# First layer's MoE routing and row transposes: VectorE in place of ScalarE and GpSimd, and another order

## The chip, the cores and the metric

The kernel runs on one core of a Trainium2 chip. Its engines work side by side, each through its own list of instructions: TensorE (PE; its weight loads are shown as PEld), VectorE (DVE), ScalarE (ACT), GpSimd (POOL) and SyncE (SP), which only starts transfers. The metric is the device time of one execution in microseconds. The kernel before took 1183.16 us, the median of three runs (1179.98, 1183.16 and 1186.79).

## The reference

A two-layer backbone over 256 latent and 256 context tokens, 512 rows of 1024 numbers in all. The first layer mixes with attention, the second with a state-space model (SSM); each is followed by a mixture of experts (MoE), in which every row goes to the best group of four and the best two of its eight experts:

```python
def moe_tokens(xt, gw, gb, rw, rb, w_gate, w_up, w_down):
    g_logits = xf @ gw + gb
    _, g_idx = lax.top_k(g_logits, 1)
    p_group = jnp.sum(softmax(g_logits) * g_onehot, axis=-1, keepdims=True)
    e_sel = jnp.einsum('sge,sg->se', e_logits, g_onehot)
    e_val, e_idx = lax.top_k(e_sel, MOE_TOP_K)
    w_top = jax.nn.softmax(e_val, axis=-1) * p_group
    ...
    hid = jax.nn.silu(xt @ w_gate) * (xt @ w_up) * combine
    return hid @ w_down
...
    h = h + m[2] * y                        # mixer's output
    h = h + m[5] * hier_moe(modulate(rms_norm(h, norm2_g[layer]), m[3], m[4]), *moe_p)
```

The rows xt that enter the experts are the normed and modulated rows: h times 1/rms, times a row a2, plus a row b2.

## The kernel before

The rows are held as four tiles of 128, t = 0 to 3. The attention's output projection makes one tile of H after another (L742 and L743), and the steps of the first layer's routing are woven in behind each tile (list at L747 to L751, pairs of step and tile). The steps are: 0 and 1 (`half`, `prep`, L834 to L853: sums of squares, 1/rms, the modulated rows xn and their transfer to `xd` in device memory), 2 (`logits` and `choose`, L858 to L906, the group and the two experts of every row), 3 (`places`, L909, each row's slot in its expert and in the last tile the index list `gidx`, L954), 4 (`worth`) and 5 (`weights`, L973 to L996, the gate weights put into a table by TensorE). For t = 0 to 2 the rows are made by VectorE (L849, L851), for the last tile by two ScalarE copies (L845), and a product and a sum of GpSimd for each half of 512 columns (L846, L847).

`gidx` lets GpSimd gather rows from `xd`: `gather(j)` (L1180) fetches the 128 slots of expert pair j, 512 KB, into one of two buffers xg0 and xg1. Between the gathers of pairs 0 and 1 stands `overflow` (L1018 to L1030), nine VectorE instructions and a memset that count the blocks of rows beyond the experts' capacity; all engines read the count (L1046) and branch on it (L1047). The branch isn't taken with these inputs.

Then 16 pairs are worked on. Of pair j, `rows` turns the gathered rows (8 transposes, L329, and two copies L1232), `up(0)` and `up(1)` are the two halves of the first product (ph, L1251), ScalarE and VectorE make the hidden values `hd` (L1259, L1260), `hidT` turns them (L1237, copy hT L1239), `down` is the second product (py, L1277) and a scatter of the result (L1280). `pipeline` (L189) runs these steps with a lag in rounds for each. In a round stand: rows of a pair, hidT and the aside work of the pair two before, up of the pair one before, down of the pair two before. The aside work is the making of the next layer's SSM matrices: VectorE products (L1610, L1611, W by a helper, L149) that wait for transfers `Rd` of GpSimd's queue, and small matmuls on TensorE (vt, kp, pk: L1624 to L1638).

Weights come as 1 MB transfers through a ring of buffers (L1334 to L1369), started by SyncE in the order of use: 13 are in flight before the branch or just behind it, the next ones wait until TensorE has finished with a buffer. Within a block a scheduler sets the order of each engine's instructions; steps written through `TE_`, `VP_`, `P_` and `A_` keep the order in which they are written.

The second layer's MoE (from about 948 us) has another scheme without gathers; its pairs keep their order.

Of the kernel before, what the change touches and what calls it, by code (L numbers as in the profile page):

```python
# [130 lines left out]
def bc(ap, shape):  # L131
    return ap.to_broadcast(shape)
# [3 lines left out]
def hybrid(ctx: ExitStack, tc: tile.TileContext, A, out, taps=None, stop=None):  # L136
    nc = tc.nc
    taps = taps or {}
    V_ = nc.vector
# [232 lines left out]
    def attention(moe_mods, disp_open):  # L372
# [350 lines left out]
        with ExitStack() as wctx:  # L723
            wq = wctx.enter_context(tc.tile_pool(name="wq", bufs=1))
            wo = Splitter(wq, [A["wout"][i] for i in range(2)], "wo", 4, (V_, nc.gpsimd))
            wo.half(0, 0)
            wo.half(0, 1)
            for hf in range(2):
                for j in range(4):
                    s = slice(j * 128, (j + 1) * 128)  # L730
                    if (hf, j) == (0, 2):
                        setup()
                    if (hf, j) == (0, 3):
                        wo.half(1, 0)
# [12 lines left out]
                    for i, t in (((0, 0),), ((1, 0), (0, 1)), ((2, 0), (1, 1), (0, 2)),  # L747
                                 ((0, 3), (1, 2), (3, 0), (4, 0), (5, 0), (2, 1)))[j]:
                        steps[i](t)
            for i, t in ((1, 3), (3, 1), (4, 1), (5, 1), (2, 2), (3, 2), (4, 2), (5, 2), (2, 3), (3, 3), (4, 3), (5, 3)):  # L750
                steps[i](t)  # L751
        octx.close()

# [50 lines left out]
    def dispatch_open(layer, Ht, M, VB, tag, xn2=None):  # L804
# [4 lines left out]
        T = M.T  # L809
# [6 lines left out]
        V_.tensor_copy(on, oneb)  # L816
        ohs = dp.tile([128, T, 32], BF, name="ohs")
        M.tabs = [bank(tag, name="ptab") for _ in range(2)]
        xns = {}

        halves = [slice(512 * i, 512 * i + 512) for i in range(2)]
        sums = dp.tile([128, T, 2], F32, name="sums")

        nt = 2 if layer == 0 else 1
        rws, C = M.scores if layer else (dp.tile([128, 8, nt, 36], F32, name="rws"), dp.tile([128, 36], F32, name="rc"))
# [7 lines left out]

        def half(t, hf):  # L834
            row_ss(sums[:, t], hf, Ht[t][:, halves[hf]])

        def prep(t):
            half(t, 1)
            turn(HT[t % 2], Ht[t], 0)
            rstd = rms(sums[:, t, 0:1], 1, D, "rstd", sums[:, t, 1:2])  # L840
            xn = dp.tile([128, D], F32, tag="xn2", bufs=2, name="xn2") if xn2 is None else xn2[:, t]
            xns[t] = rstd
            for s in halves:
                if t == T - 1:
# [64 lines left out]
        def places(t):  # L909
# [5 lines left out]
            V_.tensor_scalar(e64, m, -float(CAP), float(32 * CAP), op0=OP.mult, op1=OP.add)  # L915
            RV = M.RV[:, t]
            tm, p, ov = st("tm", [2, 32]), st("p", [2]), st("ov", [2])
            par, oj = st("par", [2]), st("oj", [2, NJ])
            ov2 = oh.rearrange("p k (a b) -> p k a b", b=per)
            if M.dma:  # L920
                V_.tensor_reduce(par, ov2[:, :, :, 1], axis=AX.X, op=OP.add)
# [10 lines left out]

            pe = st("pe", [2])
            V_.scalar_tensor_tensor(pe, in0=par, scalar=64.0 if M.dma else 1.0, in1=p, op0=OP.mult, op1=OP.add)
            eqm = st("eqm", [2, 128], FR)
            for k in range(2):
                V_.tensor_scalar(eqm[:, k], iota, pe[:, k:k + 1], None, op0=OP.is_equal)
            R = st("R", [2, 3 * NJ], FR)
            if M.dma:
                nc.gpsimd.tensor_mul(R[:, :, 0:16], oj, bc(cst[:, C_IDK + 2 * t:C_IDK + 2 * t + 2, None], [128, 2, 16]))  # L940
                for k in range(2):
# [31 lines left out]
        def weights(t):  # L973
# [19 lines left out]
            if t == T - 1:  # L993
                wt = st("wt", [N])
                nc.scalar.copy(wt, M.tabs[1][:, 0:N])
                V_.tensor_add(M.WS, wt, M.tabs[1][:, N:2 * N])  # L996
        return setup, lambda t: half(t, 0), prep, logits, choose, places, worth, weights

    def evac(mp, M, py, ws, Yh, Yl, hf):

# [16 lines left out]

    def overflow(M, e, pool):  # L1018

        nb, x, inc, one = (pool.tile([128, 32], F32, name=n) for n in ("nb", "nbx", "nbi", "nb1"))  # L1020
        CAP = M.CAP
        e.tensor_scalar(nb, M.cnt, float(CAP), None, op0=OP.is_gt)
        for i in range(1, 4):
            e.tensor_scalar(x, M.cnt, float(CAP + 128 * i), None, op0=OP.is_gt)
            e.tensor_add(nb, nb, x)
        nc.gpsimd.memset(one, 1.0)
        e.tensor_tensor_scan(inc, one, nb, 0.0, op0=OP.mult, op1=OP.add)
        tot = pool.tile([1, 1], I32, name="nbt")
        e.tensor_copy(tot, inc[0:1, 31:32])
        M.over = nb, inc, tot  # L1030

    def spill(layer, T, M, Ht, ring):

        NB, CAP = 16, M.CAP
        with ExitStack() as fctx:
# [9 lines left out]
            nb, inc, tot = M.over  # L1045
            nblk = nc.values_load(tot[0:1, 0:1], min_val=0, max_val=NB)  # L1046
            with tc.If(nblk > 0):  # L1047
                lo = st([128, 32]) if M.dma else M.a2[:, 128:160]
                V_.tensor_sub(lo, inc, nb)
                ge = fp.tile([128, NB, 32], F32, tag="ow", bufs=2, name="ge")  # L1050
                V_.tensor_tensor(ge, bc(iotb[:, 0:NB][:, :, None], [128, NB, 32]),
# [111 lines left out]
    def experts(Ht, M, VB, load, aside):  # L1163
# [3 lines left out]
        with ExitStack() as ectx:  # L1167
# [43 lines left out]
            def pair(j):  # L1211
                st = {}
# [892 lines left out]
```

## Time and profile before

| | before |
|---|---|
| median of three runs | 1183.16 us |
| the profiled execution's own time | 1182.01 us |
| its span in the trace | 1180.2 us |
| busy: PE / DVE / ACT / POOL | 77% / 53% / 30% / 23% |
| moved by DMA | 317.14 MB, 269 GB/s on the mean |

The span is the stretch from the first to the last instruction in the trace; the time of the execution is 1.8 us longer. Busy shares are means over stages with different limits. In the page, PE is busy in most slices, and the DMA engines are near full in two stretches: the first layer's MoE (about 400 to 665 us) and the second layer's (from about 948 us to the end). Between the last row of H (375.70 us) and the first gather, TensorE and the DMA engines have little to do for some 20 us, but for transfers of weights that run until about 389 us.

### The profile page before, as it was taken

Reading aid. Unit: us, or ns where it says so; the run is one execution under the profiler, and the core shown is the slowest. Engines: PE = TensorE matmul, PEld = TensorE weight load, DVE = VectorE, ACT = ScalarE, POOL = GpSimd, SP = SyncE. Lnnn points to the kernel's source line nnn. Section 1 sums busy time; section 2 is a strip of 40 time slices with the busy share of each in tenths; the row PEclk is TensorE's granted clock in tenths of the full one; section 3 lists DMA queues with packets and bytes.
Section 4 is the critical chain, followed back from the end, with each engine's and each line's share of the span. In section 5 each row is a group of like instructions: output and inputs, shape, how many; then the busy total and the mean of one; then the engine's idle time right before and its main releaser. Section 6 shows DMA issues by size and latency. Waiting matters only on the chain. (4 is left out here: it accounts for less than half of the span.)

```text
span 1180.2 us, 15033 instructions
## 1 busy us (share of the span) xinstructions
PE 913.9 (77%) x5398; PEld 477.3 (40%) x5398; DVE 625.1 (53%) x1649; ACT 350.4 (30%) x705; POOL 270.7 (23%) x347
## 2 busy tenths in 40 slices
PE   3577989999898599787897896965289597776663
PEld 0365866434487333232332245712078441121110
DVE  1778794677549516553530038988847841111113
ACT  2332224756533212111120113713754320000001
POOL 0533321322422423132126305000045300000001
PEclk9798999999999599898898997986589797788797
DMA  9782222665653699998899974382356689999994
GB/s 289 269 217 71 72 72 72 215 230 201 233 224 137 226 377 408 415 372 332 345 415 344 406 268 122 144 335 107 141 175 257 249 324 420 420 420 420 420 420 166
DMA packets 54814, 317.14 MB, mean 269 GB/s; under 512 B 8587, under 2 KB 9627, under 8 KB 21712
## 3 DMA queue, kind: packets, MB, share of 16 engines
q1 hardware_dynamic: 42910, 285.49, 63.6%
q0 software_dynamic: 10080, 26.92, 6.2%
q10 hardware_dynamic: 1746, 3.73, 0.9%
q8 instruction: 44, 0.72, 0.2%
q14 instruction: 34, 0.28, 0.1%
HBM read 305.80 MB, written 19.94 MB: 276 GB/s over the span
## 5 line engine op out<-in xcount | busy, mean ns | idle before, releaser
L1251 PE MATMUL ph<-w,xgT 128*64 128x512 f32 x512 | 140.9, 629 | 10.0 <-DMA w<-in_gu 10.0
L248 PE MATMUL pm<-wmod,cs 128*32 128x512 f32 x352 | 52.0, 683 | 60.0 <-DMA wmod<-in_modw 51.8
L339 PE MATMUL pp<-wlo,xo 128*128 128x512 f32 (+1 forms) x224 | 88.5, 395 | 5.2 <-POOL wlo L360 5.0
L338 PE MATMUL pp<-whi,xo 128*128 128x512 f32 (+1 forms) x224 | 90.0, 402 | 1.3 <-ACT whi L358 1.3
L340 PE MATMUL pp<-whi,xo 128*128 128x512 f32 (+1 forms) x224 | 87.7, 392 | 0.0
L1277 PE MATMUL py<-w,hT 128*64 128x512 f32 x224 | 76.7, 646 | 0.9 <-DMA w<-in_dn 0.8
L1251 PEld LDWEIGHTS ph<-w,xgT 128*64 128x64 f32 x512 | 38.8, 141 | 78.2 <-issue 57.8
L360 POOL TENSOR_TENSOR wlo<-win,whi 128x1024 fp32r<-128x1024 f32 (+1 forms) x20 | 44.9, 2272 | 79.5 <-ACT whi L358 79.5
L1251 PE MATMUL ph<-w,xn 128*32 128x512 f32 x256 | 43.7, 771 | 23.7 <-DMA w<-in_gu 23.6
L1260 DVE TENSOR_TENSOR a<-a,ph 128x256 f32<-128x256 f32 x8 | 3.4, 422 | 101.1 <-ACT a L1259 101.1
L339 PEld LDWEIGHTS pp<-wlo,xo 128*128 128x128 f32 x224 | 44.6, 199 | 15.6 <-POOL wlo L360 7.8
L1260 DVE TENSOR_TENSOR hd<-sg,ph 128x256 f32<-128x256 f32 x16 | 6.7, 418 | 81.4 <-ACT sg L1259 81.4
L1303 PE MATMUL py<-w,m 128*32 128x512 f32 x256 | 42.5, 747 | 9.3 <-DMA w<-in_dn 8.7
L582 DVE TENSOR_REDUCE nm<-sc 128x1 f32<-128x512 f32 (+1 forms) x64 | 35.1, 551 | 26.2 <-PE sc L615 15.7
L338 PEld LDWEIGHTS pp<-whi,xo 128*128 128x128 f32 x224 | 44.8, 200 | 10.2 <-ACT whi L358 2.2
L340 PEld LDWEIGHTS pp<-whi,xo 128*128 128x128 f32 x224 | 44.4, 198 | 8.6
L248 PEld LDWEIGHTS pm<-wmod,cs 128*32 128x32 f32 x352 | 9.4, 115 | 88.6 <-issue 48.0
L1251 PE MATMUL ph<-w,xg 128*32 128x512 f32 x256 | 32.9, 640 | 14.4 <-DMA w<-in_gu 13.1
L363 POOL TENSOR_TENSOR wlo<-glu,whi 128x512 fp32r<-128x512 f32 x16 | 26.7, 1698 | 69.4 <-ACT whi L358 67.1
L1003 DVE SCALAR_TENSOR_TENSOR Yl<-py,WS,Yh 128x512 fp32r<-128x512 f32 x18 | 13.4, 750 | 54.5 <-ACT Yh L1002 41.9
L585 ACT ACTIVATE e<-sc,nm 128x512 f32<-128x512 f32 (+1 forms) x64 | 37.4, 586 | 12.7 <-DVE nm L582 8.4
L1277 PEld LDWEIGHTS py<-w,hT 128*64 128x64 f32 x224 | 22.1, 146 | 43.5 <-issue 40.4
(492 smaller groups left out, 1953.7 us busy)
## 6 DMA issues: line engine op xcount, KB each, us to landing
w<-in_gu SPq DMA_DIRECT2D x127, 1024.0 KB
w<-in_dn SPq DMA_DIRECT2D x62, 1024.0 KB
wmod<-in_modw SPq DMA_DIRECT2D x42, 1024.0 KB
win<-in_win SPq DMA_DIRECT2D x8, 1024.0 KB
glu<-in_glu SPq DMA_DIRECT2D x8, 1024.0 KB
yd<-in_zero SPq DMA_DIRECT2D x1, 4096.0 KB
wo<-in_wout SPq DMA_DIRECT2D x4, 1024.0 KB
w<-yd SPq DMA_DIRECT2D x4, 1024.0 KB
```

The source lines that it names most:

```text
L248: nc.tensor.matmul(pm[32 * i:32 * i + 32, :], lhsT=cs[:, kk, :], rhs=w(kk), start=kk < 4, stop=kk >= 4)
L338: nc.tensor.matmul(o, lhsT=lh, rhs=rh, start=start, stop=False)
L339: nc.tensor.matmul(o, lhsT=lh, rhs=rl, start=False, stop=False)
L340: nc.tensor.matmul(o, lhsT=ll, rhs=rh, start=False, stop=stop)
L360: self.engines[i].tensor_tensor(lw, w[:, 2 * i:2 * i + 2, :], hi.bitcast(F32), op=OP.subtract)
L363: e.tensor_tensor(lw[:, k], w[:, 2 * i + k, :], hi.bitcast(F32)[:, k], op=OP.subtract)
L582: V_.tensor_reduce(nm, sp_[:, :n], axis=AX.X, op=OP.max, negate=True)
L585: nc.scalar.activation(e[:, :n], sp_[:, :n], AF.Exp, bias=nm, scale=1.0, accum_out=z)
L1003: V_.scalar_tensor_tensor(Yl[:, s], in0=py, scalar=ws, in1=Yh[:, s].bitcast(F32), op0=OP.mult, op1=OP.subtract)
L1251: nc.tensor.matmul(ph[s, :], lhsT=st["x"][:, 4 * q + kk, s], rhs=g[:, i, kk % 2] if M.dma else g[:, i], start=(q, kk) == (0, 0), stop=(q, ...
L1277: nc.tensor.matmul(py[s, :], lhsT=st["hT"][:, fk, s], rhs=d[i][:, fk, hf * 512:hf * 512 + 512], start=fk == 0, stop=fk == 1)
L1303: nc.tensor.matmul(py[s, :], lhsT=st["hT"][:, fk, s], rhs=r, start=fk == 0, stop=fk == 1)
```

## The change

1. The last tile's rows. `half` of tile 3 now also makes the product of H and a2 (VectorE, into two new tiles `xlast`), and a new step 6, `lastrows`, multiplies by 1/rms and adds b2, one VectorE instruction for each half, each half with its own transfer of 256 KB to `xd`. The copies of ScalarE and the four instructions of GpSimd are gone.
2. The order of the steps. `weights` of tiles 1 and 2 stand behind the choices of tile 3; the small tiles that they read (oj, eqm, R) have two buffers.
3. `overflow` is three VectorE instructions; the rest of the counting is inside the branch.
4. In the first MoE the `rows` of a pair stand between the two halves of `up` of the pair before, and not at the head of the round.

```diff
-            for i, t in ((1, 3), (3, 1), (4, 1), (5, 1), (2, 2), (3, 2), (4, 2), (5, 2), (2, 3), (3, 3), (4, 3), (5, 3)):
+            for i, t in ((1, 3), (3, 1), (4, 1), (2, 2), (3, 2), (4, 2), (2, 3), (6, 3), (5, 1), (3, 3), (4, 3), (5, 2), (5, 3)):
                 steps[i](t)
...
+        xlast = [sm.tile([128, 512], F32, tag=n, bufs=1, name="xlast") for n in ("mrow", "gb")] if layer == 0 else None
...
         def half(t, hf):
             row_ss(sums[:, t], hf, Ht[t][:, halves[hf]])
+            if layer == 0 and t == T - 1:
+                V_.tensor_mul(xlast[hf], Ht[t][:, halves[hf]], M.a2[:, halves[hf]])
...
             rstd = rms(sums[:, t, 0:1], 1, D, "rstd", sums[:, t, 1:2])
+            xns[t] = rstd
+            if layer == 0 and t == T - 1:
+                rstds.append(rstd)
+                return
...
+        def lastrows(t):
+            for x, s in zip(xlast, halves):
+                V_.scalar_tensor_tensor(x, in0=x, scalar=rstds[0], in1=M.b2[:, s], op0=OP.mult, op1=OP.add)
+                nc.gpsimd.dma_start(M.xd[t * 128:(t + 1) * 128, s], x)
...
-            par, oj = st("par", [2]), st("oj", [2, NJ])
+            par, oj = st("par", [2]), st("oj", [2, NJ], bufs=2 if M.dma else 1)
...
-        nb, x, inc, one = (pool.tile([128, 32], F32, name=n) for n in ("nb", "nbx", "nbi", "nb1"))
-        CAP = M.CAP
-        e.tensor_scalar(nb, M.cnt, float(CAP), None, op0=OP.is_gt)
-        for i in range(1, 4):
-            e.tensor_scalar(x, M.cnt, float(CAP + 128 * i), None, op0=OP.is_gt)
-            e.tensor_add(nb, nb, x)
-        nc.gpsimd.memset(one, 1.0)
-        e.tensor_tensor_scan(inc, one, nb, 0.0, op0=OP.mult, op1=OP.add)
-        tot = pool.tile([1, 1], I32, name="nbt")
-        e.tensor_copy(tot, inc[0:1, 31:32])
+        x, sm_, tot = pool.tile([128, 4, 32], F32, name="nbx"), pool.tile([128, 1], F32, name="nbs"), pool.tile([1, 1], I32, name="nbt")
+        e.scalar_tensor_tensor(x, in0=bc(M.cnt[:, None, :], [128, 4, 32]), scalar=float(M.CAP),
+                               in1=bc(cst[:, C_J:C_J + 4, None], [128, 4, 32]), op0=OP.subtract, op1=OP.is_gt)
+        e.tensor_reduce(sm_, x.rearrange("p a b -> p (a b)"), axis=AX.X, op=OP.add)
+        e.tensor_copy(tot, sm_[0:1])
...
-                return (rows, hidT, lambda: aside(j), lambda: up(0), lambda: back(0), lambda: up(1), lambda: back(1), down)
+                s = (rows, hidT, lambda: aside(j), lambda: up(0), lambda: back(0), lambda: up(1), lambda: back(1), down)
+                return s[1:4] + s[:1] + s[4:] if M.dma else s
...
-            pipeline([pair(j) for j in range(NJ)], (0, 2, 2, 1, 3, 1, 3, 2))
+            pipeline([pair(j) for j in range(NJ)], (2, 2, 1, 0, 3, 1, 3, 2) if M.dma else (0, 2, 2, 1, 3, 1, 3, 2))
```


The lines R and eqm have the same edit as oj; the counting that moved into the branch is not shown.

The list of GpSimd behind the last memset of a gather buffer, first before, then after. xn2 is the tile of the last rows, b2 of L1580 and L1591 a tile of SSM constants, R the gate weights' right-hand sides:

```order
L869 MEMSET xg1_3053 128x1024
L846 TENSOR_TENSOR xn2_3601<-xn2_3601,H1_95 128x512
L847 TENSOR_TENSOR xn2_3601<-xn2_3601,b2_96 128x512
L846 TENSOR_TENSOR xn2_3601<-xn2_3601,H1_95 128x512
L981 TENSOR_TENSOR R_3758<-oj_3746,wh_3768 128x2x16
L982 TENSOR_TENSOR R_3758<-oj_3746,wl_3769 128x2x16
L1580 DMA b2_96<-in_sc 128x2x128
L847 TENSOR_TENSOR xn2_3601<-xn2_3601,b2_96 128x512
L1580 DMA b2_96<-in_sc 128x2x128
L853 DMA xd0_3038<-xn2_3601 128x1024
```

The same place in the list of the changed kernel, its lines numbered 5 to 11 higher:

```order
L880 MEMSET xg1_3053 128x1024
L992 TENSOR_TENSOR R_3754<-oj_3742,wh_3869 128x2x16
L864 DMA xd0_3038<-xlast_3068 128x512
L1591 DMA b2_96<-in_sc 128x2x128
L864 DMA xd0_3038<-xlast_3069 128x512
L993 TENSOR_TENSOR R_3754<-oj_3742,wl_3870 128x2x16
L1591 DMA b2_96<-in_sc 128x2x128
L933 TENSOR_TENSOR oj_3806<-oh_3045 128x32
```

The four products and sums are gone, the transfer to `xd` is two, and both stand together with a transfer of constants ahead of the second R (wl).

TensorE's list at the first expert pairs, first before, then after. xg0 and xg1 are the gathered rows, xgT the turned rows, ph the first product:

```order
L329 MATMUL pt_4277<-cst_66,xg1_3053 128x128 x4
L329 MATMUL pt_4283<-cst_66,xg1_3053 128x128 x4
L1251 MATMUL ph_4289<-w8_3970,xgT0_4246 64x512 x4
L1251 MATMUL ph_4289<-w8_3972,xgT0_4246 64x512 x4
L1251 MATMUL ph_4289<-w8_3974,xgT0_4246 64x512 x4
L1251 MATMUL ph_4289<-w8_3976,xgT0_4246 64x512 x4
L329 MATMUL pt_4311<-cst_66,xg0_3052 128x128 x4
L329 MATMUL pt_4317<-cst_66,xg0_3052 128x128 x4
L1237 MATMUL pt_4323<-cst_66,hd0_4251 128x128 x2
```

The same place in the list of the changed kernel, its lines numbered 5 to 11 higher:

```order
L1261 MATMUL ph_4271<-w8_3970,xgT0_4243 64x512 x4
L1261 MATMUL ph_4271<-w8_3972,xgT0_4243 64x512 x4
L329 MATMUL pt_4283<-cst_66,xg1_3053 128x128 x4
L329 MATMUL pt_4289<-cst_66,xg1_3053 128x128 x4
L1261 MATMUL ph_4271<-w8_3974,xgT0_4243 64x512 x4
L1261 MATMUL ph_4271<-w8_3976,xgT0_4243 64x512 x4
L1247 MATMUL pt_4305<-cst_66,hd0_4248 128x128 x2
L1261 MATMUL ph_4309<-w8_3978,xgT1_4244 64x512 x4
L1261 MATMUL ph_4309<-w8_3980,xgT1_4244 64x512 x4
L329 MATMUL pt_4321<-cst_66,xg0_3052 128x128 x4
L329 MATMUL pt_4327<-cst_66,xg0_3052 128x128 x4
```

Of pair 1 the transposes moved from ahead of the first ph to its middle, and those of pair 2 from ahead of hidT (pt<-hd) to the middle of the next up.

The head of a later round of TensorE's list, one with aside work, first before, then after. vt<-W is the first small matmul of the aside work, W is made by VectorE:

```order
L1277 MATMUL py_4910<-w8_4901,hT1_4249 64x512
L1251 MATMUL ph_4999<-w8_5000,xgT1_4247 64x512 x4
L1624 MATMUL vt_5065<-cst_66,W_4976 128x128
L1633 MATMUL kp_5077<-W_4976,C_4870 32x64 x4
L1251 MATMUL ph_4999<-w8_5006,xgT1_4247 64x512 x4
L1624 MATMUL vt_5065<-cst_66,W_4976 128x128 x3
L1633 MATMUL kp_5077<-W_4976,C_4870 32x64 x12
```

The same place in the list of the changed kernel, its lines numbered 5 to 11 higher:

```order
L1287 MATMUL py_4907<-w8_4896,hT1_4246 64x512
L1287 MATMUL py_4907<-w8_4898,hT1_4246 64x512
L1635 MATMUL vt_5047<-cst_66,W_4958 128x128
L1261 MATMUL ph_4981<-w8_4982,xgT1_4244 64x512 x4
L329 MATMUL pt_4997<-cst_66,xg0_3052 128x128 x4
L329 MATMUL pt_5003<-cst_66,xg0_3052 128x128 x4
L1635 MATMUL vt_5047<-cst_66,W_4958 128x128 x3
```

One vt now stands ahead of the first quarter of the up, where it stood behind it; it is so in five rounds. In GpSimd's list `gather(1)` has moved too, from before the branch to the first place behind it.

## Rows read from the trace of the kernel before

**Rows 1.** The profile's page, part 4, the chain that ended last: shares by line

```profile
DMA w<-in_gu 10%; DMA w<-in_dn 7%; PE ph L1251 1%; POOL H L2072 0%; DVE Yl L1003 0%; ACT Yh L1002 0%; ACT H L2081 0%; PE py L1303 0%; PE acc L1319 0%; DVE H L2072 0%; ACT junk L317 0%; DVE a L1322 0%; DVE b L1322 0%; DVE xg L2075 0%; DVE xn
```

**Rows 2.** Busy us by stretch (length, engines, PE clock, DMA share, GB/s)

```profile
380.00:388.00 8.00, 2.25 (x14) 1.81 (x11) 8.00 (x30) 2.19 (x6) 7.30 (x9) 0.58 1.01 422
```

**Rows 3.** VectorE's instructions in order (start us, us, ...), 381 to 393 us

```profile
381.69 1.16 DVE L880 TENSOR_SCALAR pen<-gc,g 128x4 f32<-128x4 f32 x1
...
383.08 1.20 DVE L990 TENSOR_SCALAR dg<-cst,RV 128x128 fp32r<-128x128 f32 x1
...
384.30 1.14 DVE L978 TENSOR_TENSOR wl<-RV,wh 128x2 f32<-128x2 f32 x1
...
386.03 1.84 DVE L880 TENSOR_SCALAR pen<-gc,g 128x4 f32<-128x4 f32 x1
...
392.53 0.20 DVE L978 TENSOR_TENSOR wl<-RV,wh 128x2 f32<-128x2 f32 x1
```

**Rows 4.** GpSimd's instructions in order, 381 to 389 us

```profile
385.77 0.78 POOL L1580 DMA_DIRECT2D b<-in_sc  x1
...
386.57 1.27 POOL L847 TENSOR_TENSOR xn<-xn,b 128x512 f32<-128x512 f32 x1
...
388.51 0.57 POOL L853 DMA_DIRECT2D xd<-xn  x1
```

**Rows 5.** VectorE's groups over the whole span (busy us, mean ns)

```profile
L849 DVE SCALAR_TENSOR_TENSOR xn<-H,rstd,H 128x512 f32<-128x512 f32 x6 | 4.2, 747 | 0.0
...
L880 DVE TENSOR_SCALAR pen<-gc,g 128x4 f32<-128x4 f32 x6 | 3.9, 652 | 0.1
```

**Rows 6.** VectorE's instructions in order, where the routing begins and ends

```profile
375.70 0.69 DVE L743 TENSOR_TENSOR H<-H,yo 128x512 f32<-128x512 f32 x1
...
377.14 0.28 DVE L990 TENSOR_SCALAR dg<-cst,RV 128x128 fp32r<-128x128 f32 x1 [0.37 <-PE pvb L991]
...
397.48 0.17 DVE L954 TENSOR_TENSOR gidx<-zz,z 128x16 int32<-128x16 f32 x1
...
400.07 0.14 DVE L1029 CAST nbt<-nbi 1x1 int32<-1x1 f32 x1
```

**Rows 7.** GpSimd's DMA issues around the branch

```profile
399.37 1.02 POOL L1180 DMA_INDIRECT xg<-xd,gidx  x1 [0.16 <-DVE nb L1025]
...
402.53 0.57 POOL L149 DMA_DIRECT2D w<-in_gu  x1 [2.13 <-DMA b<-in_sc]
```

**Rows 8.** TensorE's work in order, first expert pairs

```profile
402.67 1.94 PE L329 MATMUL pt<-cst,xg 128*128 128x128 f32 x8 [4.57 <-DMA xg<-xd,gidx]
...
405.19 1.94 PE L329 MATMUL pt<-cst,xg 128*128 128x128 f32 x8 [0.58 <-DMA xg<-xd,gidx]
...
407.06 7.80 PE L1251 MATMUL ph<-w,xgT 128*64 128x512 f32 x32
...
414.79 1.09 PE L329 MATMUL pt<-cst,xg 128*128 128x128 f32 x8
...
417.08 0.41 PE L1237 MATMUL pt<-cst,hd 128*128 128x128 f32 x2 [1.20 <-DVE hd L1260]
```

**Rows 9.** Tile xg: time from issue to landing of its transfers

```profile
DMA to landing us min/median/max: 5.9/8.5/13.1
```

**Rows 10.** Busy us by stretch, first MoE (columns as in Rows 2)

```profile
437.00:520.00 83.00, 69.96 (x420) 27.90 (x417) 45.94 (x98) 16.68 (x34) 21.92 (x30) 0.94 1.01 409
...
543.00:546.00 3.00, 3.00 (x11) 1.02 (x9) 2.90 (x5) 0.69 (x1) 0.00 (x0) 0.66 0.15 49
...
566.00:570.00 4.00, 4.00 (x13) 1.29 (x10) 3.89 (x6) 0.77 (x2) 0.00 (x0) 0.63 0.07 12
```

**Rows 11.** TensorE's waits between 402 and 665 us (us in total, times, longest)

```profile
PE pt L1237 <- DVE hd L1260: 10.6, 5, 4.3
...
PE vt L1624 <- DVE W L149: 8.3, 3, 4.1
```

**Rows 12.** VectorE's instructions in order, 534 to 540 us

```profile
535.92 0.69 DVE L1610 TENSOR_TENSOR H<-LR,b 128x512 f32<-128x512 f32 x1 [9.28 <-DMA Rd<-H]
```

More of the change, by code (lines that the diff above doesn't have):

```diff
@@ L818, in dispatch_open @@
         M.tabs = [bank(tag, name="ptab") for _ in range(2)]
-        xns = {}
+        xns, rstds = {}, []
         halves = [slice(512 * i, 512 * i + 512) for i in range(2)]
         sums = dp.tile([128, T, 2], F32, name="sums")
+        xlast = [sm.tile([128, 512], F32, tag=n, bufs=1, name="xlast") for n in ("mrow", "gb")] if layer == 0 else None
         nt = 2 if layer == 0 else 1
@@ L840, in prep @@
             rstd = rms(sums[:, t, 0:1], 1, D, "rstd", sums[:, t, 1:2])
+            xns[t] = rstd
+            if layer == 0 and t == T - 1:
+                rstds.append(rstd)
+                return
             xn = dp.tile([128, D], F32, tag="xn2", bufs=2, name="xn2") if xn2 is None else xn2[:, t]
-            xns[t] = rstd
             for s in halves:
@@ L934, in places @@
             V_.scalar_tensor_tensor(pe, in0=par, scalar=64.0 if M.dma else 1.0, in1=p, op0=OP.mult, op1=OP.add)
-            eqm = st("eqm", [2, 128], FR)
+            eqm = st("eqm", [2, 128], FR, bufs=2 if M.dma else 1)
             for k in range(2):
                 V_.tensor_scalar(eqm[:, k], iota, pe[:, k:k + 1], None, op0=OP.is_equal)
-            R = st("R", [2, 3 * NJ], FR)
+            R = st("R", [2, 3 * NJ], FR, bufs=2 if M.dma else 1)
             if M.dma:
@@ L996, in weights @@
                 V_.tensor_add(M.WS, wt, M.tabs[1][:, N:2 * N])
-        return setup, lambda t: half(t, 0), prep, logits, choose, places, worth, weights
+        return (setup, lambda t: half(t, 0), prep, logits, choose, places, worth, weights) + ((lastrows,) if layer == 0 else ())
     def evac(mp, M, py, ws, Yh, Yl, hf):
@@ L1018, in overflow @@
     def overflow(M, e, pool):
-        nb, x, inc, one = (pool.tile([128, 32], F32, name=n) for n in ("nb", "nbx", "nbi", "nb1"))
-        CAP = M.CAP
-        e.tensor_scalar(nb, M.cnt, float(CAP), None, op0=OP.is_gt)
-        for i in range(1, 4):
-            e.tensor_scalar(x, M.cnt, float(CAP + 128 * i), None, op0=OP.is_gt)
-            e.tensor_add(nb, nb, x)
-        nc.gpsimd.memset(one, 1.0)
-        e.tensor_tensor_scan(inc, one, nb, 0.0, op0=OP.mult, op1=OP.add)
-        tot = pool.tile([1, 1], I32, name="nbt")
-        e.tensor_copy(tot, inc[0:1, 31:32])
-        M.over = nb, inc, tot
+        x, sm_, tot = pool.tile([128, 4, 32], F32, name="nbx"), pool.tile([128, 1], F32, name="nbs"), pool.tile([1, 1], I32, name="nbt")
[3 more added lines that the diff above has]
+        e.tensor_copy(tot, sm_[0:1])
+        M.over = x, tot
     def spill(layer, T, M, Ht, ring):
@@ L1044, in spill @@
                 overflow(M, V_, fp)
-            nb, inc, tot = M.over
+            x4, tot = M.over
             nblk = nc.values_load(tot[0:1, 0:1], min_val=0, max_val=NB)
@@ L1048, in spill @@
                 lo = st([128, 32]) if M.dma else M.a2[:, 128:160]
+                nb, inc, one = (st([128, 32]) if M.dma else M.a2[:, 160 + 32 * i:192 + 32 * i] for i in range(3))
+                V_.tensor_reduce(nb, x4.rearrange("p a b -> p b a"), axis=AX.X, op=OP.add)
+                V_.memset(one, 1.0)
+                V_.tensor_tensor_scan(inc, one, nb, 0.0, op0=OP.mult, op1=OP.add)
                 V_.tensor_sub(lo, inc, nb)
```

## The prediction

> **What bounds the kernel now.** I read the chain that ended last first: what it names are the weight transfers of the second layer's MoE [rows 1]. So the end of the kernel is bound by DMA from about 948 us on; a change in the first layer counts only by how much earlier that stretch begins. I then read the stretch that the change touches by busy time: between 380 and 388 us VectorE is busy all 8.00 us, GpSimd 7.30, TensorE 2.25 [rows 2]. TensorE waits there for VectorE, and the first gather waits for `gidx`, which VectorE writes at 397.48, 21.8 us after the last sum of H at 375.70 [rows 6]. The place is thus on the path, and VectorE is its bound. In the first MoE behind it the DMA engines are full for most of the time (409 GB/s from 437 to 520), but fall to 49 and 12 GB/s for 3 and 4 us [rows 10]. TensorE has waits of its own there, 10.6 us for `hd` and 8.3 for W [rows 11]. So an earlier start is passed on whole as far as TensorE, which frees the ring's buffers, starts earlier; inside the MoE small shifts of TensorE are partly hidden by the full queue and partly not.
>
> **What goes in the routing.** Four VectorE instructions take far longer than their size asks for: pen, dg, wl, pen with 1.16, 1.20, 1.14 and 1.84 us [rows 3]. All four fall under GpSimd's products and sums of 128x512, four of 1.27 us like the one shown [rows 4], and each ends as one of those ends (386.03 + 1.84 = 387.87, 386.57 + 1.27 = 387.84). Usual durations: pen, the other four of its group, (3.9 - 1.16 - 1.84)/4 = 0.23; dg 0.28 [rows 5, 6]; wl 0.20 [rows 3]. The excess is 0.93 + 1.61 + 0.92 + 0.94 = 4.4 us. With GpSimd's four instructions gone it goes: -4.4.
>
> The Trainium skill ("SBUF — State Buffer", section "Who interferes with whom") has this as a lock: a VectorE instruction with two SBUF inputs stands still while a GpSimd instruction that reads SBUF runs. The row of wl agrees: 1.14 us beside a GpSimd product, 0.20 without. The same rule holds for the two new VectorE instructions, which read two SBUF tiles each, beside GpSimd's remaining small products of R; by it the sum would be some tenths worse, which is inside my bounds.
>
> **What comes.** Two scalar_tensor_tensor of 128x512; six of the same form take 0.747 us each [rows 5]: +1.5, an upper bound, since instructions overlap by some hundredths at their ends. Two products of 128x512 at 0.69 (the sum of H is of that form [rows 6]). The one of the first half is made long before, while VectorE waits for the projection; the one of the second half stands right behind the last sum of H, and the idle time of 0.37 before the dg at 377.14, which waits for TensorE [rows 6], takes up part of it: 0.69 - 0.37 = +0.3. ScalarE's two copies are off the path. Sum of VectorE's work: -4.4 + 1.5 + 0.3 = -2.6.
>
> **What is late next.** In the changed list GpSimd has a transfer to `xd` (0.57), one of constants (0.78) and a second to `xd` (0.57) between the two R of tile 1's weights [rows 4]. TensorE's table product needs the second R, and VectorE's second dg of that tile needs a buffer that TensorE frees behind it. With VectorE now faster this chain is likely to be late: 0 at best, 0.57 + 0.78 + 0.57 = 1.9 at worst. I take the middle, +1.0. Behind that dg on VectorE stand the choices and places of the last tile, and for them waits TensorE, so the whole of it counts. Routing in all: -1.6, between -2.6 (or -3.0, if the new instructions overlap) and +0.3, which would be 1.9 of wait and some more for constants that land late for the product brow, which is now nearer to its transfer.
>
> The moved `weights` of tiles 1 and 2 are the same instructions as before and are done in VectorE's and GpSimd's shadows; moved ahead of nothing that `gidx` needs, they cost 0. The transfers to `xd` now start some 4 us earlier than 388.51 and land long before the gather.
>
> **The branch and the second gather.** `overflow` ends at 400.07, 2.4 us behind `gidx` (397.65); three instructions in place of nine save an estimated 1.1 (four pairs of compare and add become one of four times the width). Both gathers stood before that. Now gather(1) is issued behind the branch, where GpSimd issued its first transfer at 402.53, that is 4.9 behind `gidx` [rows 7], less 1.1: 3.8, in place of 1.7 (399.37). The first gather lands before TensorE's 402.67, 5.0 behind `gidx`, and that is not moved, so the earlier branch gives nothing. The second is needed only behind the first half of the first up. That up began at 407.06, 9.4 behind `gidx`, held by the transposes of pair 1 (1.94 from 405.19 [rows 8]), which now move into it: start 8.4, first half 3.9, needed at 12.3. Issued at 3.8 it lands at 9.6 with the 5.8 us of before (399.37 to 405.19), at 12.3 with the median of all gathers, 8.5, and at 16.9 with the longest, 13.1 [rows 9]. I take 0, bounds 0 and +4.6.
>
> **Turned rows among the products.** First round: the up starts 1.0 earlier, the 8 transposes inside it take about 1.1 (as at 414.79), and those of pair 2 no longer fill the wait before hidT, so its idle time grows from 1.20 to some 2.3 [rows 8]; hidT stands where it stood: 0. In later rounds hidT has 1.1 us less cover and may wait that much more for `hd`, but the same 1.1 us is gone from that place of the list: 0 where `hd` is late for another reason, and +1.1 where `hd` follows this round's products. In five rounds a vt that needs W stands ahead of the first quarter of an up; a quarter is 7.80 / 4 = 1.95 us [rows 8]. So W late by that much, which was covered, is now waited for: 0 to 5 x 1.95 = +9.8. On the other side the copy of xgT and the gather's buffer come earlier than VectorE's wait for Rd (9.28 us at 535.92 [rows 12]), and the two dips of the DMA stream, worth 3 x (1 - 49/409) + 4 x (1 - 12/409) = 6.5 us [rows 10], could close: -6.5. W's own waits were 8.3 us in three places [rows 11], not in every round, and the queue is full around them, so I take 0 as the nearest to what the rows bear out.
>
> **Sum.** -1.6 + 0 + 0 on the profiled execution's 1182.01 gives 1180.4. Its median stands 1.15 above it (1183.16), so I forecast 1181.5, which is no change as this kernel can be measured: 0.5% or 5.9 us, that is from 1177.2 to 1189.1.
>
> The Trainium skill ("SBUF — State Buffer", section "SBUF: two separate sides") also says that GpSimd cannot write its transfers' descriptors while VectorE runs an instruction in a mode that uses the shared port. That speaks against this change, which puts VectorE work of 128x512 beside four GpSimd transfers. The issue of 0.78 at 385.77 beside 0.57 at 388.51 doesn't contradict it. By it the chain of three issues would grow by up to one VectorE instruction each; the rival below named "hidden" has the price from rows.
>
> **Rivals.**
> - *The dips close* (faster). The routing gives -2.6, no new wait, and the stream keeps full: -6.5. 1182.0 - 9.1 + 1.15 = 1174. For it: xgT's copy and the second Rd transfers stand earlier in the lists. Against: the waits for Rd themselves are landings of transfers, 9.28 us long, which the new order doesn't shorten. 0.18.
> - *W ahead of the up* (slower). TensorE stands before vt for a whole quarter in five rounds, +9.8, and frees each ring buffer as much later: 1182.0 - 1.6 + 9.8 + 1.15 = 1191. It comes out slower than can be told from no change once the wait is over 1.5 us a round. For it: waits for W up to 4.1 us in one place [rows 11]. Against: in the other places W is in time. 0.15.
> - *Gather(1) late*: +4.6 - 1.6 = +3.0: 1186. For it the longest landing [rows 9]; against, nothing but this gather and one transfer of weights runs then. 0.12.
> - *Hidden*: the issue chain on GpSimd (1.9) and the constants' landing take all of it, or the branch decides: 1183. 0.13.
> - The forecast, 0.42, with its own range of 1179 to 1184.
>
> Chances: faster by over 0.5% 0.21 (the first rival and a little of the forecast's spread), slower 0.16, no change 0.63. The range of 1174.5 to 1188.5 leaves out half of the first and most of the second rival.
>
> **What would show it.** In the changed kernel's trace: pen, dg and wl of 1.1 to 1.8 us gone between 380 and 388; `gidx` about 20.2 us behind the last sum of H; one new wait of about 1 us of a dg for pvb; gather(1) issued about 4 us behind `gidx` and TensorE not waiting for it; hidT's idle time up by about 1 in the first round; in the five rounds little idle time ahead of the first vt, and the two dips still there. I am wrong if `gidx` comes less than 0.5 or more than 3.5 us earlier, if TensorE waits for xg in the middle of the first up, or if the stretch from the first up to the last weights of the first MoE changes by over 3 us.

## The result: 1.2% slower, and the profile after

| | before | after |
|---|---|---|
| median | 1183.24 us (1179.98 to 1186.79, four runs) | 1196.21 us (1195.28 to 1198.99, four runs) |
| the profiled execution's own time | 1182.01 us | 1195.28 us |
| its span | 1180.2 us | 1193.5 us |
| TensorE's idle time ahead of hidT in the first MoE | 10.6 us [rows 11] | 20.8 us |

The ratio is 1.0124, with a 95% interval from 1.0093 to 1.0155. A second set of five runs gave 1193.51 us, 1.0095 (1.0059 to 1.0131).

**The routing** did most of what was forecast, and lost it again in one wait. VectorE in order, from the last sum of H to `gidx` (start us, duration, line, operation, tiles; in brackets the idle time before and what ended it):

```profile
376.56 0.69 DVE L743 TENSOR_TENSOR H<-H,yo 128x512 f32<-128x512 f32 x1
...
381.65 0.53 DVE L891 TENSOR_SCALAR pen<-gc,g 128x4 f32<-128x4 f32 x1
...
383.09 0.74 DVE L863 SCALAR_TENSOR_TENSOR xlast<-xlast,rstd,b 128x512 f32<-128x512 f32 x1
...
384.20 0.75 DVE L863 SCALAR_TENSOR_TENSOR xlast<-xlast,rstd,b 128x512 f32<-128x512 f32 x1
...
385.08 0.15 DVE L989 TENSOR_TENSOR wl<-RV,wh 128x2 f32<-128x2 f32 x1
...
385.25 0.22 DVE L891 TENSOR_SCALAR pen<-gc,g 128x4 f32<-128x4 f32 x1
...
392.83 0.69 DVE L1621 TENSOR_TENSOR brow<-LR,b 128x512 f32<-128x512 f32 x1 [3.09 <-DMA b<-in_sc]
...
397.94 0.17 DVE L965 TENSOR_TENSOR gidx<-zz,z 128x16 int32<-128x16 f32 x1
```

The reader is to see that pen takes 0.53 and 0.22 us and wl 0.15, where 1.16, 1.84 and 1.14 stood [rows 3], and that the two new instructions (L863) cost 0.74 and 0.75. But a product of the SSM work (L1621, `brow`) stands 3.09 us for constants `b` to land, with the last tile's choices queued behind it. From the last sum of H to `gidx` it is 21.38 us, where it was 21.78 [rows 6].

GpSimd's transfers there, the second load of constants and the two gathers:

```profile
386.22 0.76 POOL L1591 DMA_DIRECT2D b<-in_sc  x1
...
398.39 1.12 POOL L1190 DMA_INDIRECT xg<-xd,gidx  x1 [1.65 <-DVE WS L1007]
402.00 1.53 POOL L1190 DMA_INDIRECT xg<-xd,gidx  x1 [2.49 <-DVEq L1053]
```

The load was issued at 386.22 and held the product until 392.83, 6.6 us. Gather(1) now starts at 402.00, behind the branch, 3.9 behind the end of `gidx` (398.11). TensorE takes that without a wait:

```profile
402.99 1.94 PE L329 MATMUL pt<-cst,xg 128*128 128x128 f32 x8 [4.44 <-DMA xg<-xd,gidx]
406.16 5.29 PE L1261 MATMUL ph<-w,xgT 128*64 128x512 f32 x16 [1.23 <-ACT xgT L1242]
411.38 1.09 PE L329 MATMUL pt<-cst,xg 128*128 128x128 f32 x8
...
417.00 0.44 PE L1247 MATMUL pt<-cst,hd 128*128 128x128 f32 x2 [0.94 <-DVE hd L1270]
```

The turned rows of pair 1 (411.38) follow the first half of the up at once, and hidT of pair 0 begins at 417.00, where it was 417.08 [rows 8]. So at this point the change has neither lost nor won anything. The 13 us are lost later.

**The first MoE.** TensorE's waits from 402 to 680 us (us in all, times, longest), then VectorE's:

```profile
PE pt L1247 <- DVE hd L1270: 20.8, 5, 8.3
PE vt L1635 <- DVE W L149: 9.7, 3, 4.5
```

```profile
DVE brow L1621 <- DMA b<-in_sc: 25.2, 2, 15.2
...
DVE H L1621 <- DMA b<-in_sc: 14.4, 1, 14.4
```

The wait for `hd` has doubled [rows 11], its longest from 4.3 to 8.3 us; that for W has grown by 1.4 only. VectorE now waits for loads of constants, `b` from `in_sc`, up to 15.2 us at once. The stretch of the long waits (length, PE, PEld, DVE, ACT, POOL busy, granted clock, DMA share, GB/s), after and then before:

```profile
520.00:600.00 80.00, 61.39 (x318) 22.39 (x320) 38.27 (x81) 13.53 (x26) 14.66 (x19) 0.85 0.78 304
```

```profile
520.00:600.00 80.00, 68.80 (x381) 25.29 (x378) 41.51 (x81) 15.16 (x31) 16.89 (x21) 0.91 0.89 348
```

The DMA engines move 304 GB/s in place of 348: the dips of [rows 10] have grown. One round of it, on VectorE of the changed kernel:

```profile
522.00 0.42 DVE L1249 COPY hT<-pt 128x256 f32<-128x256 f32 x1 [0.53 <-PE pt L1247]
...
545.87 0.69 DVE L1621 TENSOR_TENSOR H<-LR,b 128x512 f32<-128x512 f32 x1 [14.43 <-DMA b<-in_sc]
...
547.08 0.41 DVE L1270 TENSOR_TENSOR hd<-sg,ph 128x256 f32<-128x256 f32 x1
548.27 0.42 DVE L1249 COPY hT<-pt 128x256 f32<-128x256 f32 x1 [0.78 <-PE pt L1247]
```

VectorE works in order. L1621 is the first product of the *next* group of SSM constants; the scheduler has put it ahead of this round's `hd` (L1270). It stands 14.43 us for its transfer, and `hd` with it, and behind `hd` hidT on TensorE (idle for 7.87 us ahead of 547.55), the ring's buffers and the weights. The kernel before has the same two products ahead of `hd` in the same three rounds; 9.28 us of wait at [rows 12] is one of them. What differs is GpSimd's list. After, and then before:

```profile
528.24 1.02 POOL L1290 DMA_INDIRECT yd<-Y,sidx  x1 [3.53 <-ACT Y L1289]
530.66 1.12 POOL L1190 DMA_INDIRECT xg<-xd,gidx  x1 [1.40 <-PE pt L329]
531.79 0.58 POOL L1625 DMA_DIRECT2D Rd<-H  x1
...
532.92 0.71 POOL L1591 DMA_DIRECT2D b<-in_sc  x1
```

```profile
522.35 1.34 POOL L1280 DMA_INDIRECT yd<-Y,sidx  x1 [1.80 <-ACT Y L1279]
525.74 0.74 POOL L1580 DMA_DIRECT2D b<-in_sc  x1 [2.06 <-DVE tm L1611]
526.47 0.57 POOL L1614 DMA_DIRECT2D Rd<-H  x1
527.04 0.55 POOL L1614 DMA_DIRECT2D Rd<-b  x1
...
535.14 1.07 POOL L1180 DMA_INDIRECT xg<-xd,gidx  x1 [7.02 <-PE pt L329]
```

The group that the product waits for is two `Rd` transfers, which free its room, and the load of `b`. Before, the gather stood 8 us behind the group; now it is issued directly ahead of it, since the rows whose transposes free its buffer are turned earlier in the round. Before's hT in these rounds:

```profile
517.80 0.42 DVE L1239 COPY hT<-pt 128x256 f32<-128x256 f32 x1
...
539.89 0.42 DVE L1239 COPY hT<-pt 128x256 f32<-128x256 f32 x1 [0.18 <-PE pt L1237]
```

The middle one of the three rounds, from one hT to the next in us, worked out from these rows and, for the last three columns, from rows of experiments below (group: the two `Rd` and the load of `b`):

| | before | after | constants first | gathers 8 to 13 behind | changed, old order of pairs (e1) |
|---|---|---|---|---|---|
| hT to the group's first issue | 7.9 | 9.8 | 9.9 | 8.6 | 8.6 |
| to the product's start | 10.2 | 14.1 | 12.8 | 11.7 | 12.3 |
| to the next hT | 4.0 | 2.4 | 3.7 | 3.6 | 3.8 |
| round | 22.1 | 26.3 | 26.4 | 23.9 | 24.6 |

There are three such rounds; together they take 65.1 us before (498.57 to 563.68) and 76.3 after (499.33 to 575.64). These 11.2 us are nearly all of the loss between the two traces. In the first of the three the transfers take little longer (9.3 us from issue to product; 7.8 before, 9.6 in e1); there the gather waits 5.69 us for TensorE's transposes, ahead of 509.44, and the group behind it is issued 3.2 us later. So the gather costs in two ways: GpSimd works in order too, and the group's transfers land later.

### The profile page after: what moved, and what is told of

Its sections match the earlier page's. It is cut to its first block, busy times and chain, and to the rows that moved or that the text cites. A ratio compares the mean times of both kernels' runs of the same rounds, so it can differ in the third digit from the quotient of the medians.

```text
span 1193.5 us, 14997 instructions
## 1 busy us (share of the span) xinstructions
PE 924.7 (77%) x5398; PEld 478.3 (40%) x5398; DVE 621.4 (52%) x1641; ACT 349.3 (29%) x703; POOL 267.1 (22%) x342
## 5 line engine op out<-in xcount | busy, mean ns | idle before, releaser
L1261 PE MATMUL ph<-w,xgT 128*64 128x512 f32 x512 | 135.7, 633 | 9.1 <-DMA w<-in_gu 7.7
L1261 PEld LDWEIGHTS ph<-w,xgT 128*64 128x64 f32 x512 | 35.5, 142 | 72.7 <-issue 52.9
L1270 DVE TENSOR_TENSOR a<-a,ph 128x256 f32<-128x256 f32 x8 | 3.4, 421 | 99.3 <-ACT a L1269 99.3
L1313 PE MATMUL py<-w,m 128*32 128x512 f32 x256 | 45.2, 799 | 8.0 <-DMA w<-in_dn 7.3
L338 PEld LDWEIGHTS pp<-whi,xo 128*128 128x128 f32 x224 | 44.7, 200 | 10.1 <-ACT whi L358 2.2
L582 DVE TENSOR_REDUCE nm<-sc 128x1 f32<-128x512 f32 (+1 forms) x64 | 35.0, 551 | 26.3 <-PE sc L615 15.9
L1289 ACT ACTIVATE Y<-py,WS 128x512 f32<-128x512 f32 x28 | 19.2, 688 | 85.4 <-PE py L1287 81.9
```

Source lines behind the costliest of these rows:

```text
L338: nc.tensor.matmul(o, lhsT=lh, rhs=rh, start=start, stop=False)
L582: V_.tensor_reduce(nm, sp_[:, :n], axis=AX.X, op=OP.max, negate=True)
L1261: nc.tensor.matmul(ph[s, :], lhsT=st["x"][:, 4 * q + kk, s], rhs=g[:, i, kk % 2] if M.dma else g[:, i], start=(q, kk) == (0, 0), stop=(q, ...
L1289: nc.scalar.activation(Y[:, hf * 512:hf * 512 + 512], py, AF.Copy, scale=M.WS[:, j:j + 1])
L1313: nc.tensor.matmul(py[s, :], lhsT=st["hT"][:, fk, s], rhs=r, start=fk == 0, stop=fk == 1)
```

## The experiments

Three theories of the loss. **A**: the new place of the rows moves the gather ahead of the group, the product hoisted ahead of `hd` waits longer, and TensorE behind it. **B**: TensorE's own new order costs (less cover ahead of hidT, vt for W ahead of the up). **C**: the routing, the branch or the late gather(1) costs.

**The parts apart.** `e1_old_pair_order` has the change without part 4, `e2_pair_order_alone` part 4 alone:

```diff
-                return s[1:4] + s[:1] + s[4:] if M.dma else s
+                return s
-            pipeline([pair(j) for j in range(NJ)], (2, 2, 1, 0, 3, 1, 3, 2) if M.dma else (0, 2, 2, 1, 3, 1, 3, 2))
+            pipeline([pair(j) for j in range(NJ)], (0, 2, 2, 1, 3, 1, 3, 2))
```

> The changed kernel with the steps of a pair in their old order (part 4 undone; routing, last rows and overflow as changed). Theory T1: the 13 us are lost in the first MoE, because VectorE's hd stands behind a product of the SSM constants that waits for their load (b from in_sc), which the new order of GpSimd's list issues behind a scatter, a gather and two Rd transfers; with the old pair order that order goes, hidT waits about 10 us in all as before, and the time is 1183 +- 2. Rival T2: TensorE's own order costs it (transposes amid the up, a vt for W ahead of it): also 1183, the run does not part T1 from T2. Rival T3: the routing and the branch cost it (brow waits 3.09 us for constants, gather(1) issued 2 us later): 1192 or more.

> The kernel before with the new order of a pair's steps alone (part 4 alone). T1 and T2: 1195 +- 2, with waits of L1610 for b from in_sc of 10 to 15 us in three rounds and hidT waiting about 20 us for hd. T3: 1184 or less.

Measured: e1 1185.41 us, 1.0046 (1.0024 to 1.0069) of the kernel before; e2 1195.66 us, 1.0130 (1.0110 to 1.0149). Part 4 alone makes the whole loss. Parts 1 to 3 alone cost some too, where no change was expected: in e1 TensorE waits 7.9 us in two places for gathered rows (5.2 before), since gather(1) stands behind the branch and the old order needs it early; `brow` waits 2.89 us there. The parts don't add up: with the new order TensorE's wait for gathered rows is 4.4 us in one place, so the late gather is hidden there.

**The product tied to its place.** `VP_` keeps the order in which steps are written, so the product comes behind `hd`. TensorE's list stays the same. `e3_inorder_after` is the changed kernel so, `e4_inorder_before` the one before:

```diff
-                        V_.tensor_mul(x, L[0], C[r])
+                        VP_.tensor_mul(x, L[0], C[r])
```

> The changed kernel, with the product x of the SSM readout (L1621) tied behind VectorE's work written ahead of it, so that it is no longer drawn forward ahead of hd of the round before; everything else as changed, TensorE's order with the transposes amid the up too. T1: hidT's wait for hd falls from 20.8 to under 3 us and the time falls by 10 us or more, to 1185 or less. T2: hidT's waits fall but the time stays within 3 us of 1196. The GpSimd list keeps the load of b behind a scatter and a gather.

> The kernel before with the same tie (L1610). T1: its hidT waits (10.6 us for hd, in five places) go too, and as the two dips of the DMA stream (6.5 us) hang on them the time falls by 4 to 9 us, to 1174 to 1179. T2 has no reason for a change: 1183 +- 2.

Measured: e3 1170.21 us, 0.9921 (0.9905 to 0.9937); e4 1171.61 us, 0.9927 (0.9910 to 0.9943). TensorE's waits and the stretch from 520 us in e3:

```profile
PE py L1287 <- DMA w<-in_dn: 19.4, 17, 2.3
PE ph L1261 <- DMA w<-in_gu: 8.7, 8, 1.4
PE pt L1247 <- DVE hd L1270: 1.9, 2, 0.9
```

```profile
520.00:600.00 80.00, 70.30 (x377) 25.52 (x379) 39.02 (x76) 15.22 (x30) 14.68 (x19) 1.00 1.02 418
```

The wait for `hd` is gone (1.9 us), the stream full (418 GB/s, clock 1.00), and TensorE waits for weights instead. Over all sets of runs the changed kernel gains 23 to 26 us from one letter, the one before 8 to 10. With the wait gone the two take the same time, so the whole loss went through it, as A says; what the gather has to do with it is tried below. B falls as the cause: e3 keeps TensorE's order, and in the round shown hidT (547.55) starts as `hd` ends (547.49), so less work ahead of hidT costs nothing there. C falls too, as e3 keeps the routing and the branch.

**The other two of the four, and all on the same runs.** `e5_old_pairs_tied` is e1 with the product tied, `e7_new_pairs_tied` e2 with it; `e14` to `e16` repeat e3, e5 and e4 beside each other.

> The changed kernel with the old order of a pair's steps and the product x of the readout tied as in e3. It takes the changed routing without the turned rows' new place, and without the product brow waiting for constants in the routing. If the late gather(1) and brow's wait are what made e1 slower than the kernel before: brow's wait is gone, gather(1) still lands after the old order wants it, so the first hT comes 1 to 3 us later than in e3 and the time is 1171 to 1174. If the turned rows gain or cost nothing by themselves: the same as e3, 1170.

> The kernel before with the new order of a pair's steps and the tie of e4, without the changed routing. Against e3 it gives the routing's worth with no wait of hd: if the routing gains the 2 to 4 us that the first hT shows between e3 and e4, 1172 to 1174. Against e4 (1171.6) it gives the worth of the turned rows: T2 would have it 5 us or more slower than e4; T1 within 2 us.

> The changed kernel with the product tied to its place, again, now beside the two other tied kernels on the same runs: 1169 to 1172 us. If the new place of the rows costs something of its own once nothing stands ahead of hd, it is slower than the tied kernel with the old order of pairs by 1 us or more; if not, within 0.5 us.

> New routing, old order of pairs, product tied: 1168 to 1171 us, the fastest of the three tied kernels.

> The kernel before with the product tied: 1170 to 1173 us. Against the tied kernel with the new routing and the old order of pairs it shows what the routing part alone is worth: 2 to 3 us by the 3.3 us between the last sum of H and gidx, 0 if the stream of weights hides it.

Measured: e5 1169.41 us, 0.9889 (0.9861 to 0.9916); e7 1174.31 us, 0.9916 (0.9889 to 0.9943). Together: e14 1170.53 us, 0.9893 (0.9866 to 0.9920), e15 1172.43 us, 0.9916 (0.9889 to 0.9942), e16 1171.79 us, 0.9922 (0.9893 to 0.9952). e5 looked best in its own set of runs, and e15, the same kernel, was expected to be the fastest; but on equal runs the tied kernels can't be told apart. The last sum of H to `gidx` is 18.07 us in e3 against 21.34 in e4, so the routing is 3.3 us shorter where `brow` doesn't wait; the time shows at most 1 or 2 of them. TensorE waits there for weights from a full stream (418 GB/s in e3), which fits, though no run shows that this takes the rest.

**Which place in GpSimd's list.** `e6_constants_by_act` issues the load of `b` from ScalarE, `e10_constants_first` writes it ahead of the two Rd (list: gather, b, Rd, Rd), `e12_gather_behind` holds the gathers from pair 6 on behind the group, and `e13_gathers_8_to_13_behind` those of pairs 8 to 13 alone. The edits of e6, e10 (here the line that moved) and e13:

```diff
-                        nc.gpsimd.dma_start(cells[:, q % 2], A["sc"][:, :, q * NG:q * NG + NG, :])
+                        nc.scalar.dma_start(cells[:, q % 2], A["sc"][:, :, q * NG:q * NG + NG, :])
...
                     for r in range(2):
+                    if q + 2 < 64 // NG:
+                        loadc(q + 2)
...
-                nc.gpsimd.indirect_dma_start(out=M.xg[j % 2], out_offset=None, in_=M.xd,
+                (P_ if 7 < j < 14 else nc.gpsimd).indirect_dma_start(out=M.xg[j % 2], out_offset=None, in_=M.xd,
```

> The changed kernel with the load of b (in_sc) issued by ScalarE's queue, no longer behind scatter, gather and Rd on GpSimd's; L1621 still stands ahead of hd. If it is the place of that load in GpSimd's list that made the change slow: L1621's waits for b (39.6 us in all) are replaced by shorter ones for Rd (some 25 us, 7 to 11 each, as before) and the time falls to 1180 to 1186. If the loads are slow wherever they are issued, or TensorE's order is the cause: 1193 or more.

> The changed kernel with the load of b (in_sc) written ahead of the two Rd transfers of its round, on the same GpSimd queue; TensorE's list and the place of L1621 ahead of hd stay. If the load's place behind the Rd transfers made the three rounds of 23, 26 and 27 us (hT to hT) in the changed kernel: they shrink to 20 to 24 and the time falls by 5 to 9 us, to 1185 to 1189. If the wait for Rd takes the load's place at the same length, or TensorE's order is the cause: within 3 us of the changed kernel (1193.5 to 1196).

> The changed kernel with each gather from pair 6 on held behind the two Rd transfers of its round on GpSimd's queue (order: load of b, Rd, Rd, gather); TensorE's list is the same, and L1621 stays ahead of hd. After e10 (load of b ahead of Rd: nothing gained, 1195) and e6 (load on another queue: a third gained), theory T1 is narrowed: the gather of 512 KB, which the turned rows' new place puts right ahead of the group, delays whichever transfer L1621 waits for. If so, the three rounds of 23 to 27 us shrink to 20 to 24 (in all by 6 to 11 us) and the time is 1184 to 1190. If the gather is not the cause (TensorE's order with its lesser cover ahead of hidT, or the landing times are long whatever the order): within 3 us of 1193.5 to 1196.

> The changed kernel with the gathers of pairs 8 to 13 alone held behind the two Rd transfers (the run before this one held all from pair 6 on, and its gathers of pairs 6, 14 and 15 came late: TensorE waited 4.3 us for xg at 482 and 12.2 us at 650). If these late gathers made the rest of that kernel's gap, this one takes 1181 to 1185 us, as the kernel before. If the rest comes from the rows' new place itself (less work ahead of hidT, a later scatter ahead of the group), it stays at 1186 to 1189.

Measured: e6 1191.20 us, 1.0071 (1.0044 to 1.0097), above what was expected. Its three rounds take 67.5 us (504.82 to 572.36), with the gather still ahead of the two Rd, so there 8.8 of the 11.2 us are back; but in the three rounds ahead of them the product waits 10.1, 10.2 and 8.8 us for the load, which takes 10.6 to 11.7 us from issue to product, where the changed kernel's group took 8.0 to 9.7. e10 1195.26 us, 1.0109 (1.0079 to 1.0139): nothing gained. e12 1188.99 us, 1.0047 (1.0024 to 1.0070), and e13 1189.26 us, 1.0047 (1.0020 to 1.0074). In e10 the product waits for Rd instead; VectorE, then GpSimd:

```profile
524.91 0.42 DVE L1249 COPY hT<-pt 128x256 f32<-128x256 f32 x1 [0.78 <-PE pt L1247]
...
547.60 0.69 DVE L1625 TENSOR_TENSOR H<-LR,b 128x512 f32<-128x512 f32 x1 [13.17 <-DMA Rd<-H]
...
551.27 0.42 DVE L1249 COPY hT<-pt 128x256 f32<-128x256 f32 x1 [0.78 <-PE pt L1247]
```

```profile
533.72 1.07 POOL L1190 DMA_INDIRECT xg<-xd,gidx  x1 [1.40 <-PE pt L329]
534.79 0.75 POOL L1588 DMA_DIRECT2D b<-in_sc  x1
535.54 0.58 POOL L149 DMA_DIRECT2D Rd<-H  x1
```

It waits 13.17 us ahead of 547.60 for the first Rd, issued at 535.54. So the load's place within the queue is nothing; whatever lands last of the group holds the product. In e13 the gather stands behind:

```profile
521.39 0.42 DVE L1249 COPY hT<-pt 128x256 f32<-128x256 f32 x1 [0.78 <-PE pt L1247]
...
541.66 0.69 DVE L1621 TENSOR_TENSOR H<-LR,b 128x512 f32<-128x512 f32 x1 [10.17 <-DMA Rd<-H]
...
545.28 0.42 DVE L1249 COPY hT<-pt 128x256 f32<-128x256 f32 x1 [0.78 <-PE pt L1247]
```

```profile
528.62 1.32 POOL L1290 DMA_INDIRECT yd<-Y,sidx  x1 [4.51 <-ACT Y L1289]
529.95 0.74 POOL L1591 DMA_DIRECT2D b<-in_sc  x1
...
532.09 1.07 POOL L149 DMA_INDIRECT xg<-xd,gidx  x1 [0.30 <-issue]
```

The three rounds take 69.3 us (499.84 to 569.12), 7.0 of the 11.2 us are back. The late gathers of e12 (TensorE waited 21.2 us for gathered rows in it, 4.4 in e13) were not the rest of its gap, as had been held possible.

Against the kernel before, the gather ahead of the group is thus some 60% of the loss in these traces. But e13 has parts 1 to 3 too, and the kernel that differs from it by the pairs' order alone is e1. VectorE there:

```profile
523.10 0.42 DVE L1249 COPY hT<-pt 128x256 f32<-128x256 f32 x1 [0.18 <-PE pt L1247]
...
543.97 0.69 DVE L1620 TENSOR_TENSOR H<-LR,b 128x512 f32<-128x512 f32 x1 [12.03 <-DMA Rd<-H]
...
547.72 0.42 DVE L1249 COPY hT<-pt 128x256 f32<-128x256 f32 x1 [0.18 <-PE pt L1247]
```

Its three rounds take 69.2 us (501.80 to 570.99), as long as e13's, and the ratios of the times are equal too, 1.0046 and 1.0047. So with the gathers behind the group the new place of the rows costs nothing more in these rounds, and the 4 us that are left are there in the old order as well. In the whole time some 3 us may be left to it, since e1 also waits longer for gathered rows (7.9 us, 4.4 in e13). In e1's round the scatter `yd` is issued directly ahead of the group (530.35, then 531.65), as in e13 and in the last of the three rounds before (547.04, then 548.43, and 11.6 us to the product); in the round of before that is shown it stands 3.4 us ahead. Whether that is why wasn't tried alone, and e1's trace is of an execution 3.8 us above its median: rounds of the same order differ by 4 us from trace to trace.

**The gathers ahead of the branch.** `e9_gathers_first` is e5 with gather(0) and gather(1) written ahead of `overflow`, `e11_gathers_first_new_pairs` the same of e3:

```diff
+                for j in range(2):
+                    nc.gpsimd.indirect_dma_start(out=M.xg[j], out_offset=None, in_=M.xd,
```

> e5 (changed routing, old order of a pair's steps, product x tied) with gather(0) and gather(1) both written ahead of the overflow count, so that gather(1) is issued before the branch again. If gather(1) behind the branch is what holds e5's start (8.3 us of waits for xg in two places against 4.6 in e4): the first hT comes 2.5 to 4 us sooner behind the last sum of H than in e5 (41.2 us there), and the time is 1165 to 1168 where e5 had 1169.4. If the DMA stream hides it: 1169.

> e3 (changed kernel, product x tied) with both gathers ahead of the branch as in e9. TensorE did not wait for the second gather in e3, so 1170 as e3, within 1 us; against e9 it gives the price of the turned rows with equal gathers: 1 to 4 us slower than e9.

Measured: e9 1171.07 us, 0.9901 (0.9871 to 0.9932), a miss, the gain didn't come: the first hT starts 40.3 us behind the last sum of H, 0.9 sooner than in e5 and not 2.5 to 4. e11 1171.01 us, 0.9905 (0.9877 to 0.9932), as e3, as expected, but not the 1 to 4 us slower than e9 that were expected too. **The changed kernel as it is, again** (`e8_changed_again`) gave the 1193.51 us above, 1.0095, below the expected 1.012 to 1.014.

> The changed kernel as it is, for comparison on the same chip: 1.012 to 1.014 times the kernel before, as e2, since part 4 alone made all of the loss there.

## Why the prediction was wrong

- *What goes, -4.4*: right; pen, pen, dg and wl took 4.2 us less (0.53, 0.22, 0.28 and 0.15). The pen of 0.53 ends at 382.18, and a memset of GpSimd beside it at 382.16. By the Trainium skill ("SBUF — State Buffer", section "Who interferes with whom") a VectorE instruction with two SBUF inputs contends with a GpSimd instruction that reads SBUF. The row of wl agrees: without GpSimd's products beside it, it fell from 1.14 to 0.15 us.
- *What comes, +1.8*: right (0.74, 0.75 and one product more).
- *What is late next, +1.0, bounds 0 and 1.9*: the place was wrong. The dg that I named didn't wait, and GpSimd's three issues took 0.59, 0.73 and 0.57 us (384.13 to 386.01) beside the two new VectorE instructions, no longer than before. The constants on the same queue held `brow` for 3.09 us, which I had only as "some more" and in the rival *Hidden*, with a chance of 0.13. The routing gave 0.4 and not 1.6.
- *The branch and gather(1), 0*: right; issued 3.9 behind the end of `gidx` (forecast 3.8), and TensorE didn't wait for it.
- *Turned rows among the products, 0*: this step failed: the three rounds took 11.2 us more, and part 4 alone made the time 1.3% longer (e2). In the first round hidT's idle time was 0.94 us and not some 2.3. I priced it on TensorE's list alone (cover ahead of hidT, vt for W), and let it touch VectorE's wait for Rd only as a gain: "the copy of xgT and the gather's buffer come earlier than VectorE's wait". The rows also release the gather, 512 KB on the queue on which that wait's transfers stand. What the runs showed: the gather now ahead of them, the product's wait up from 9.28 to 14.43 us in the middle round, and `hd` and hidT behind it; with the product tied behind `hd` (e3) the loss is gone, and with the gathers behind (e13) the three rounds take as long as in the old order (e1). I had the wait [rows 12] and the dips [rows 10], and had written that the waits are landings of transfers, but did not ask which transfers now stand ahead of these.
- *Rivals*: "W ahead of the up" named 1191, near the time measured, for a reason that did not occur (W's waits 9.7 against 8.3 us). "The dips close" came out the other way round: they grew.

## What to carry to other kernels

An engine that works in order passes a transfer's landing on to all that stands behind the waiting instruction: before moving a step, look for instructions ahead of the critical one that end in a wait for DMA, and list what the step puts ahead of that transfer on its queue. Where such a wait is seen in the trace of before, it is a lever of its own: tying one product to its place gave 8 to 10 us to the old kernel and 23 to 26 to the changed one, more than the whole change was about. Compare close variants on the same runs: the kernel before moved by 4 us from one set to another, and with it a gain of 2 to 4 us appeared that was not there on equal runs. Compare with the kernel that differs by the one part, too: against the kernel before, the gather seemed 60% of the loss in the three rounds, against e1 all of it.

## What the runs showed of the hardware

In the second and third of the rounds the same three transfers of GpSimd took, from the first issue to the release of the product, 12.2 to 14.6 us with the gather of 512 KB directly ahead of them (changed kernel, e10) and 10.2 to 12.3 without (before, e1, e13); in the first round 9.3 and 11.0 against 7.8 to 10.0. And TensorE came back slow from the long waits. Granted clock (behind the five busy columns) before, in and behind the wait at 547.5 us, changed kernel:

```profile
536.00:540.00 4.00, 3.68 (x13) 1.03 (x12) 0.00 (x0) 0.65 (x2) 0.00 (x0) 1.00 1.01 382
540.00:547.50 7.50, 0.00 (x0) 0.00 (x0) 1.62 (x3) 0.00 (x0) 0.00 (x0) 0.67 0.94 387
547.50:549.00 1.50, 1.45 (x4) 0.59 (x6) 0.73 (x3) 0.00 (x0) 0.00 (x0) 0.50 0.06 22
```

It is 1.00 (2.4 GHz) in the busy stretch, and 0.50 (1.2 GHz) for the hidT behind 7.5 us of idle time.
